# Seven-product x projections in the scan, with the sums of u kept on chip and gates and output halves staged in DRAM

## The chip, the cores and the metric

The kernel runs on one core of a Trainium2 chip. The metric is the device time of one execution in microseconds (us). Instructions of a core run on five engines with queues of their own: TensorE (PE, matmuls; PEld its weight loads), VectorE (DVE), ScalarE (ACT), GpSimd (POOL, here only an issuer of DMAs) and SyncE (SP, the issuer of the weight loads from DRAM).

## The reference

One layer of a hybrid decoder trunk over 512 tokens and 16 meta tokens (L = 528), width 1024, float32:

```python
u = rmsnorm(h, mix_norm_w[i])
proj = u @ w_in[i]              # 1024 x (1024 pool, 2048 z, 4096 xbc, 32 dt, 2048 gates)
gates = sigmoid(proj[..., OFF_GATE:] + b_gate[i])
y_pool = pool_mixer(u_pool, pool_w_group[i], pool_scale[i]) @ w_pool_up[i]
y_ssd = mamba2_branch(z, xbc, dt_raw, ...) @ w_ssd_out[i]    # 8 groups of 4 heads
h = h + (gate_pool * y_pool + gate_ssd * y_ssd) @ w_o[i]
v = rmsnorm(h, mlp_norm_w[i])
hid = relu(v @ w_ff1[i])
h = h + (hid * hid) @ w_ff2[i]
out = rmsnorm(h, final_norm_w)
```

In `mamba2_branch` each group has a B and a C tile of 128 columns, two x tiles of 128 and two z tiles. B, C and x go through a causal convolution of width 4 and a silu before the chunked scan.

## The kernel before

**Numbers as high and low parts.** Every float32 operand of a large matmul is split into a rounded part (ACT copy, `whi`) and the remainder (DVE subtraction, `wlo`). A product is three matmuls per 128-slice of the contraction: high by high, high by low, low by high.

**Stages.** (1) Squares, dt and the projections of group 0, with `first_raw` copies and the first four pool gates (`gate_pool(d, True)`); `norm_u` writes the normalised u as `uh` and `ul` (8 tiles each) and a copy to DRAM (`u_d`). (2) The scan: for each group g of 8, `ssd(g)` is interleaved by `weave` with the projections of group g+1 (`group_proj`), in group 4 also with the first half of the output product (`out_half`, contraction over ys 0 to 7), in group 7 with a further part (`out_part`). (3) The pool: two plain tiles, the last output slices (`psl`), then three pool pairs by seven products (`pool_pair`). (4) The merge of the branches and the output projection, (5) the MLP. In stages 4 and 5 products of 2 x 2 blocks are also formed by seven products in place of eight.

**Seven products.** Contraction and output columns are each cut in two, and so are the tokens. Seven products of sums of blocks, added up in the right order, replace eight block products. They need sums of the blocks of u (`sums_of_u`), and sums of the weight blocks. The latter are made by DMAs that accumulate in DRAM (`weight_sums`, on POOL's queue; a set of four sums is 8 DMAs, a set of two is 4), at the places given by `SETS_AT` (by group), `SETS_POOL` and a loop behind the merge. The sums of u are formed during groups 1, 2, 3 and 5 (`SUMS_AT`), written to DRAM (`t_d`) and loaded again ahead of the pool (`T`).

**Projections in the scan.** A plain tile (`proj`) multiplies 8 slices of a weight block with both halves of the tokens: 16 matmuls by `uh`, 16 by `ul`, 16 with `wlo`, each 264 columns wide (258 for C). The result lies in a PSUM tile of two banks (`psum2`, two such tiles) from which `conv` reads it. z and gate tiles are 512 columns wide.

**Order.** Each engine runs its instructions in one fixed order, which a list scheduler lays down when the kernel is built, by program order and its own times; `tc.issue_after(x)` keeps an instruction behind x. Weight blocks pass through three `raw`, four `whi` and four `wlo` buffers.

**Kept on chip.** Eight gate tiles `m1` (pool gates, 512 columns) and eight accumulators `acc` (the output product, 512 columns) lie in SBUF from the start of the scan or before. `out_half` copies into `acc` (ACT, line 636), `out_part` adds to it (DVE, line 665), `psl` adds the rest (line 898).

Of the kernel before, what the change touches and what calls it, by code (L numbers as in the profile page):

```python
# [47 lines left out]
SKIP = 8  # L48
TN = (L - SKIP) // 2

SUMS_AT = (1, 2, 3, 5)


SETS_AT = {0: 2, 1: 1, 3: 1, 5: 1, 6: 1}
# [9 lines left out]
def kernel(ctx: ExitStack, tc, xT, x, w, f1, f2, vec, fnw, out):  # L64
# [10 lines left out]
    nblk = [0]  # L75
# [66 lines left out]
    sel = const.tile([P, 2, P], F32, name="sel")  # L142
    dve.tensor_copy(sel[:, 0, :], ident[:, P - 1 : P].to_broadcast([P, P]))
    dve.tensor_copy(sel[:, 1, :], ident[:, NM - 1 : NM].to_broadcast([P, P]))
# [20 lines left out]

    gc_stack = ExitStack()
    gc = gc_stack.enter_context(tc.tile_pool(name="gc", bufs=2, side="left", reuse_waits="tile"))
    m1p = ctx.enter_context(tc.tile_pool(name="m1p", bufs=1, side="right", reuse_waits="tile"))
    m1 = [m1p.tile([P, SEQ], F32, tag=f"m1_{d}", name=f"m1_{d}") for d in range(NK)]
# [56 lines left out]
    wdt = pre.tile([P, NK, H], F32, name="wdt")  # L226
# [63 lines left out]
    dts_ = pre.tile([P, L], F32, name="dtp")  # L290
# [80 lines left out]
    def dt_out():  # L371

        pt = psum1("pt_dt")
# [17 lines left out]

    u_d = [dram.tile([P, 2 * TN], F32, name=f"u_d{k}") for k in range(NK)]

    def norm_u():
        for k in range(NK):
            dve.scalar_tensor_tensor(xt[k], xt[k], col(V_MIX, k), rsb, op0=ALU.mult, op1=ALU.mult)
            nc.gpsimd.dma_start(u_d[k], xt[k][:, SKIP:])
            act.copy(uh[k], xt[k])
            dve.tensor_tensor(ul[k], xt[k], uh[k].bitcast(F32), op=ALU.subtract)
# [19 lines left out]
    def first_raw(name, ps, skip):  # L419
        r = pre.tile([P, L - skip], F32, tag="raw0", name=f"raw0_{name}", bufs=4)  # L420
        act.copy(r, ps)
        dve.tensor_tensor(r, r, rsb[:, skip:], op=ALU.mult)
        return r

    def group_proj(g, cur, gate=None):
# [3 lines left out]
        for dst, t, skip in ((bt, 16 + g, 0), (ct, 24 + g, NM - 4), (xc[:, 0, :], 2 * g, 0),  # L429
                             (xc[:, 1, :], 2 * g + 1, 0)):  # L430
# [6 lines left out]
            yield  # L437
# [4 lines left out]
        for i in range(2):  # L442

            with tc.issue_after(done[0].ins) if g == 1 else nullcontext():
                wt = block()
            proj(narrow(ps[:, i * SEQ : (i + 1) * SEQ]), wt, X if first else U)
# [150 lines left out]

    def gate_pool(d, first=False):
        ps = psum2(f"pgp{d}")[:, :SEQ]
        proj(narrow(ps), block(), X if first else U)  # L600
        if first:
            dve.tensor_tensor(m1[d], ps, rsb[:, NM:], op=ALU.mult)
        act.activation(m1[d], m1[d] if first else ps, AF.Sigmoid, bias=col(V_BG, d))
# [17 lines left out]
    acc_stack = ExitStack()  # L621
    accp = acc_stack.enter_context(tc.tile_pool(name="accp", bufs=1, side="right", reuse_waits="tile"))
    acc = [accp.tile([P, SEQ], F32, tag=f"acc{d}", name=f"acc{d}") for d in range(NK)]
# [7 lines left out]
    def out_half():  # L631
        for dd in range(4):
            ps = psum2(f"pso{dd}")
            for i in range(2):
                ssd_out(2 * dd + i, ps[:, i * SEQ : (i + 1) * SEQ], range(8))
                act.copy(acc[2 * dd + i], ps[:, i * SEQ : (i + 1) * SEQ])
                yield

    def out_part():
# [24 lines left out]
        def add(ps, d):  # L664
            dve.tensor_tensor(acc[d], acc[d], ps, op=ALU.add)
# [14 lines left out]
        for d in range(2, NK):  # L680
# [8 lines left out]
    ts_stack = ExitStack()  # L689
    tsp = ts_stack.enter_context(tc.tile_pool(name="tsp", bufs=1, side="right", reuse_waits="tile"))  # L690
    t_d = {(n, p, k): dram.tile([P, 2 * TN], F32R, name=f"t_d{n}{p}{k}")
           for n in ("13", "42") for p in "hl" for k in range(4)}
    one, two = slice(0, TN), slice(TN, 2 * TN)

    B11, B12, B22, B21 = range(4)
    sets = [("f2", 0), ("f2", 1), ("f1", 0), ("f1", 1), ("f1", 2), ("f2", 2), ("f2", 3), ("f1", 3),
            ("f2", 4), ("f1", 4), ("f2", 5), ("f1", 5), ("f2", 6)]
    assert len(sets) == f1.shape[0] + f2.shape[0]  # L700
    SUMS = {"f1": ("t1", "s3", "t2", "t4"), "f2": ("t1", "s3")}
# [4 lines left out]
    def weight_sums():  # L706
        t = sets.pop(0)
        src = {"f1": f1, "f2": f2}[t[0]][t[1]]
# [22 lines left out]
    def sums_of_u(k, g):  # L731
        a, b = (tsp.tile([P, 2 * TN], F32, tag=t, name=f"{t}{k}") for t in ("ua", "ub"))

        with tc.issue_after(abc_load[g].ins):
            for t, kk in ((a, k), (b, k + 4)):
                sums_load[g] = nc.gpsimd.dma_start(t, u_d[kk])
        yield
        with tc.issue_after(masked[g].ins):
            dve.tensor_tensor(a[:, one], a[:, two], a[:, one], op=ALU.subtract)
            dve.tensor_tensor(a[:, two], b[:, two], a[:, two], op=ALU.subtract)  # L740
            dve.tensor_tensor(b[:, two], b[:, two], a[:, one], op=ALU.subtract)
            dve.tensor_tensor(b[:, one], b[:, one], b[:, two], op=ALU.subtract)
        yield
        for src, n in ((a, "13"), (b, "42")):
            hi, lo = (tsp.tile([P, 2 * TN], F32R, tag=f"t{p}", name=f"t{p}{n}{k}") for p in "hl")
            if n == "42":
                yield
            with tc.issue_after((y_first if n == "13" else squared)[g].ins):
                act.copy(hi, src)
            dve.tensor_tensor(lo, src, hi.bitcast(F32), op=ALU.subtract)  # L750
            nc.gpsimd.dma_start(t_d[n, "h", k], hi)
            nc.gpsimd.dma_start(t_d[n, "l", k], lo)
            yield

    for g in range(G):
# [4 lines left out]
        if g in SUMS_AT:  # L760
            fill.append(sums_of_u(SUMS_AT.index(g), g))
# [5 lines left out]
    ts_stack.close()  # L767


    gp_stack = ExitStack()  # L770
    gtp = gp_stack.enter_context(tc.tile_pool(name="gtp", bufs=2, side="left", reuse_waits="tile"))
    pool_stack = ExitStack()
    gp = pool_stack.enter_context(tc.tile_pool(name="gp", bufs=2, side="left", reuse_waits="tile"))
    tf = pool_stack.enter_context(tc.tile_pool(name="tf", bufs=1, side="left", reuse_waits="tile"))
# [34 lines left out]
    def pool_pair(p, behind=None):  # L809

        a1, a2 = raw_block(), raw_block()
        sm = tf.tile([P, 1024], F32, tag="sm", name=f"sm{p}")
# [3 lines left out]
        with tc.issue_after(behind[0].ins) if behind[0] is not None else nullcontext():  # L816
            dve.tensor_tensor(sm[:, h1], a2[:, h1], a2[:, h2], op=ALU.add)
        with tc.issue_after(behind[1].ins) if behind[1] is not None else nullcontext():
            dve.tensor_tensor(sm[:, h2], sm[:, h1], a1[:, h1], op=ALU.subtract)
        fs = split_form(sm, both, f"S{p}")  # L820
        dve.tensor_tensor(a1[:, h1], a1[:, h1], a2[:, h1], op=ALU.subtract)
        dve.tensor_tensor(a1[:, h2], a1[:, h2], sm[:, h2], op=ALU.subtract)
# [3 lines left out]
        x = psum2(f"pxx{p}")[:, :TN]  # L826
        y, z = (psum1(f"p{i}{p}")[:, :TN] for i in "yz")
        c1, c2 = slice(SKIP, SKIP + TN), slice(SKIP + TN, L)
        u1, u2 = (lambda k: (uh[k][:, c1], ul[k][:, c1])), (lambda k: (uh[k][:, c2], ul[k][:, c2]))
        form = lambda n, c: lambda k: (T[n, "h", k][:, c], T[n, "l", k][:, c])  # L830

        def product(*a):
            with tc.issue_after(last[p].ins) if p in last else nullcontext():
                multiply(*a)

        def multiply(ps, wf, c, f, start, stop, k0=0):
            for low in range(2):
                for k in range(4):
                    wt = wf[low][:, 512 * c + k * P : 512 * c + (k + 1) * P]
                    bh, bl = f(k0 + k)  # L840
                    last[p] = pe.matmul(ps, wt, bh, start=start and not low and k == 0,
                                        stop=stop and low == 1 and k == 3, skip_group_check=True)
                    if not low:
                        pe.matmul(ps, wt, bl, start=False, stop=False, skip_group_check=True)

        product(x, fa, 0, u1, True, False)
        act.copy(r1[:, c1], x)
        product(y, fa, 1, u1, True, True, 4)
        dve.tensor_tensor(r1[:, c1], r1[:, c1], y, op=ALU.add)
        product(x, fs, 1, form("42", two), False, False)  # L850
        act.copy(r1[:, c2], x)
        product(z, fs, 0, form("13", one), True, False)
        copied[p] = act.copy(r2[:, c2], z)
        product(x, fd, 0, form("13", two), False, False)
        dve.tensor_tensor(r2[:, c2], r2[:, c2], x, op=ALU.add)
        product(z, fd, 1, u2, False, True, 4)
        dve.tensor_tensor(r1[:, c2], r1[:, c2], z, op=ALU.add)
        first = averaged(2 * p, r1)
        product(x, fb, 1, form("42", one), False, True)
        act.copy(r2[:, c1], x)  # L860
        return [first, averaged(2 * p + 1, r2)]
# [55 lines left out]
    pool_stack.close()  # L917
    wo_stack = ExitStack()
# [735 lines left out]
```

## Time and profile before

| | |
|---|---|
| median of 3 runs | 1001.25 us (1000.6 to 1002.03) |
| profiled execution | 1001.49 us |
| its span, first to last instruction | 999.8 us |
| granted TensorE clock | 1.000 |
| PE busy | 991.7 us, 6095 matmuls |
| DVE, ACT, POOL busy | 790.8, 602.6, 88.3 us |
| scan, groups 0 to 7 | about 69 to 478 us |
| pool | about 478 to 558 us |

The profile is of one execution. Rows of instructions give a line of the kernel, the engine, the operation, the tile written and the tiles read, a count, the busy time and the mean duration; behind the bar stands the engine's idle time before them and what ended it. A line can be that of a helper. A matmul's own duration includes its way through the array; how fast matmuls follow one another is read from their starts, or from the chain, where each step counts only its part.

### The profile page before, as it was taken

The numbers are of one execution on the slowest core, as the hardware profiler recorded it, in microseconds if no ns is written. First come the engines' busy times: TensorE is split into PE (matmuls) and PEld (weight loads), VectorE is DVE, ScalarE is ACT, GpSimd is POOL, SyncE is SP. The second block draws the span as 40 slices with busy tenths as digits, with TensorE's granted clock in tenths as the row PEclk, the third lists the DMA queues.
The fourth block names the chain that finished last, engine by engine and source line by source line (L and its number), as shares of the span: only waits on it lengthen the run. The fifth ranks groups of instructions, "written<-read, shape, count | busy, mean of one in ns | idle before, by whom it ended". The sixth has DMA issues, their size and how long they took to land.

```text
span 999.8 us, 15519 instructions
## 1 busy us (share of the span) xinstructions
PE 991.7 (99%) x6095; PEld 879.2 (88%) x6095; DVE 790.8 (79%) x1141; ACT 602.6 (60%) x832; POOL 88.3 (9%) x148
## 2 busy tenths in 40 slices
PE   9999999999999999999999999999999999999997
PEld 7889999999889999988998888888889999999986
DVE  7988797979736687978789566976988888888885
ACT  8675958595827339483265433378666656656654
POOL 0022101111002011003210001121100000000000
PEclk9999999999999999999999999999999999999999
DMA  7378753677238635408988622879654455464432
GB/s 244 91 281 233 222 159 117 202 181 240 68 92 259 162 108 147 148 22 237 277 198 246 214 95 90 226 200 306 168 189 148 152 186 152 144 189 149 127 106 85
DMA packets 56203, 171.47 MB, mean 172 GB/s; under 512 B 6401, under 2 KB 7745, under 8 KB 55105
## 3 DMA queue, kind: packets, MB, share of 16 engines
q1 hardware_dynamic: 36576, 105.86, 32.4%
q0 software_dynamic: 18832, 63.71, 24.4%
q8 instruction: 48, 0.79, 0.3%
q10 hardware_dynamic: 720, 0.91, 0.3%
q14 instruction: 27, 0.21, 0.1%
HBM read 161.90 MB, written 48.40 MB: 210 GB/s over the span
## 4 chain that ended last, share of the span: by engine, by line
PE 96%; ACT 2%; DMA 0%; issue 0%; DVE 0%; SPq 0%; ACTq 0%
PE px L192 12%; PE px L1289 8%; PE alpha L1357 6%; PE px L194 6%; PE pz L192 5%; PE px L1292 4%; PE alpha L1360 3%; PE pgs L192 3%; PE pgp L192 3%; PE pz L194 3%; PE py L554 2%; PE po L548 2%; PE pf L128 1%; PE pf L127 1%; PE wo_alpha L1051 1%; PE pgp L194 1%
## 5 line engine op out<-in xcount | busy, mean ns | idle before, releaser
L93 ACT CAST whi<-raw 128x1024 fp32r<-128x1024 f32 (+2 forms) x98 | 98.5, 1015 | 105.3 <-PE px L194 31.8
L95 DVE TENSOR_TENSOR wlo<-raw,whi 128x1024 fp32r<-128x1024 f32 (+2 forms) x98 | 114.6, 1176 | 52.4 <-ACT whi L93 26.9
L192 PE MATMUL px<-uh,whi 128*128 128x264 f32 (+1 forms) x448 | 113.6, 291 | 0.0
L194 PE MATMUL px<-ul,whi 128*128 128x264 f32 (+1 forms) x448 | 110.7, 285 | 0.0
L192 PEld LDWEIGHTS px<-uh,whi 128*128 128x128 f32 x448 | 84.6, 189 | 1.8 <-issue 1.4
L194 PEld LDWEIGHTS px<-ul,whi 128*128 128x128 f32 x448 | 84.3, 188 | 0.4 <-issue 0.2
L1064 DVE TENSOR_TENSOR ht<-ht,alpha 128x1024 f32<-128x1024 f32 x35 | 42.7, 1219 | 29.1 <-PE alpha L1357 29.1
L987 ACT CAST shi<-rawf 128x1024 fp32r<-128x1024 f32 x42 | 44.2, 1053 | 28.6 <-PE alpha L1360 18.2
L192 PE MATMUL px<-uh,wlo 128*128 128x264 f32 (+1 forms) x448 | 58.5, 283 | 0.0
L192 PEld LDWEIGHTS px<-uh,wlo 128*128 128x128 f32 x448 | 55.9, 188 | 0.0
L1357 PE MATMUL alpha<-shi,hh 128*128 128x512 f32 x140 | 55.2, 394 | 0.0
L1360 PE MATMUL alpha<-shi,hl 128*128 128x512 f32 x140 | 54.7, 391 | 0.0
L988 DVE TENSOR_TENSOR slo<-rawf,shi 128x1024 fp32r<-128x1024 f32 x42 | 51.2, 1218 | 0.6 <-ACT shi L987 0.6
L1292 PE MATMUL px<-vsl,shi 128*128 128x256 f32 x192 | 47.4, 280 | 0.0
L1289 PE MATMUL px<-vsh,shi 128*128 128x256 f32 x192 | 47.4, 281 | 0.0
L194 PE MATMUL pz<-ul,whi 128*128 128x512 f32 x112 | 43.6, 389 | 0.0
L192 PE MATMUL pz<-uh,whi 128*128 128x512 f32 x112 | 43.6, 389 | 0.0
L575 DVE RECIPROCAL rs<-rs 128x128 f32<-128x128 f32 x32 | 27.2, 910 | 14.0 <-ACT rs L573 13.9
L1357 PE MATMUL alpha<-slo,hh 128*128 128x512 f32 x140 | 37.4, 389 | 0.0
L1289 PEld LDWEIGHTS px<-vsh,shi 128*128 128x128 f32 x192 | 36.2, 188 | 0.9
L1292 PEld LDWEIGHTS px<-vsl,shi 128*128 128x128 f32 x192 | 36.1, 188 | 0.9
L1292 PE MATMUL px<-vl,shi 128*128 128x256 f32 x144 | 36.1, 283 | 0.0
(558 smaller groups left out, 2856.8 us busy)
## 6 DMA issues: line engine op xcount, KB each, us to landing
raw<-in_w SPq DMA_DIRECT2D x104, 512.0 KB, 4.5
f_t<-in_f POOLq DMA_DIRECT2D x38, 512.0 KB, 6.6
f_s<-in_f POOLq DMA_DIRECT2D x26, 512.0 KB, 8.6
b<-in_f SPq DMA_DIRECT2D x21, 512.0 KB, 4.6
rawf<-in_f SPq DMA_DIRECT2D x36, 256.0 KB, 3.0
rawf<-f_t SPq DMA_DIRECT2D x36, 256.0 KB, 2.9
abc<-acs_d POOLq DMA_DIRECT2D x8, 1024.0 KB, 7.5
f_t<-f_t POOLq DMA_DIRECT2D x12, 512.0 KB, 4.4
```

Of the source, the lines that this page charges most:

```text
L93: act.copy(hi[:, c], raw[:, c])
L95: dve.tensor_tensor(lo[:, c], raw[:, c], hi[:, c].bitcast(F32), op=ALU.subtract)
L192: pe.matmul(o, wt, rhs[0][k][:, c], start=part == 0 and k == 0, stop=part == 1 and k == NK - 1)
L194: pe.matmul(o, wt, rhs[1][k][:, c], start=False, stop=False)
L575: dve.reciprocal(rs[:, ctok(c)], rs[:, ctok(c)])
L987: splits.append((act.copy(hi, src), dve.tensor_tensor(lo, src, hi.bitcast(F32), op=ALU.subtract)))
L988: dve.tensor_tensor(lo, src, hi.bitcast(F32), op=ALU.subtract)))
L1064: added[0] = dve.tensor_tensor(o, o, src, op=op)
L1289: pe.matmul(ps, m, f[k][0], start=start and not low and k == 0, stop=stop and low == 1 and k == 3, skip_group_check=True)
L1292: pe.matmul(ps, m, f[k][1], start=False, stop=False, skip_group_check=True)
L1357: pe.matmul(ps[t], hh[:, p, seg, st], m, start=bool(first and not low and p == 0), stop=bool(last and low and p == 1), skip_group_check=True)
L1360: pe.matmul(ps[t], hl[:, p, seg, st], m, start=False, stop=False, skip_group_check=True)
```

## The change

- The sums of u are formed during groups 0, 1 and 2 (two slices in group 2) in another arrangement of the seven products, with token halves of 264 in place of 260, and stay in SBUF (16 tiles `T`) up to the pool. The stores to and loads from `t_d` go.
- The two x tiles of groups 4 to 7 (projected during groups 3 to 6) are computed together by seven products (`pair`). Two PSUM banks take turns; ACT copies and DVE adds bring the products into two SBUF tiles (`ra`, `rb`), from which `conv` then reads both tiles. Two more weight sets (`fx`) of four sums each are formed, in groups 0 and 1; the other sets move back.
- Pool gates 0 to 6 and the output halves pass through a two-buffer staging tile (`gt`) to DRAM (`gate_d`, `acc_d`). The parts of group 7 are added by an accumulating DMA in place of the DVE add. After the scan `acc` and `m1` are loaded from DRAM.
- In group 0 the raw copies have three buffers for four, one shared with the dt product; the selection matrix is built later.

```diff
-SKIP = 8
-TN = (L - SKIP) // 2
-SUMS_AT = (1, 2, 3, 5)
-SETS_AT = {0: 2, 1: 1, 3: 1, 5: 1, 6: 1}
+SUMS_AT = {0: (0,), 1: (1,), 2: (2, 3)}
+X_PAIRS = (4, 5, 6, 7)
+BC_PAIRS = ()
+PAIRS = [(k, g) for g in range(G) for k in "bx" if g in (BC_PAIRS if k == "b" else X_PAIRS)]
+SETS_AT = {0: 1, 1: 1, 2: 1, 3: 1, 4: 1, 5: 1, 6: 1}
...
+    gtp = gp_stack.enter_context(tc.tile_pool(name="gtp", bufs=2, side="left", reuse_waits="tile"))
...
+    T = {(n, p, k): tf.tile([P, L], F32R, name=f"t{n}{p}{k}") for n in "01" for p in "hl" for k in range(4)}
...
-    m1 = [m1p.tile([P, SEQ], F32, tag=f"m1_{d}", name=f"m1_{d}") for d in range(NK)]
+    gate_d = [dram.tile([P, SEQ], F32, name=f"gate_d{d}") for d in range(NK)]
+    acc_d = [dram.tile([P, SEQ], F32, name=f"acc_d{d}") for d in range(NK)]
...
+    def factor_u(name):
+        if name in ("A11", "A12", "A22"):
+            o = 0 if name == "A11" else 4
+            c = HF[1] if name == "A22" else HF[0]
+            return [(uh[o + k][:, c], ul[o + k][:, c]) for k in range(4)]
+        n, c = {"S1": ("1", HF[1]), "S2": ("0", HF[0]), "S3": ("0", HF[1]), "S4": ("1", HF[0])}[name]
+        return [(T[n, "h", k][:, c], T[n, "l", k][:, c]) for k in range(4)]
+
+    MULTIPLY = (("b11", "A11", 0, True, False), ("b21", "A12", 1, True, True), ("t2", "S2", 0, False, False),
+                ("t1", "S1", 1, True, False), ("s3", "S3", 0, False, False), ("b22", "S4", 1, False, True),
+                ("t4", "A22", 0, False, True))
...
+    def pair(kind, g, r):
+        ps = psum2(f"pq{kind}{g}")
+        banks = (ps[:, :HALF], ps[:, 512 : 512 + HALF])
+        operands = pair_operands(PAIRS.index((kind, g)))
+        one, two = HF
+        for m, f, n, start, stop in MULTIPLY:
+            o = banks[n]
+            wt = next(operands)
+            f = factor_u(f)
+            for low in range(2):
+                for k in range(4):
+                    wk = wt[low][:, k * P : (k + 1) * P]
+                    pe.matmul(o, wk, f[k][0], start=start and not low and k == 0,
+                              stop=stop and low == 1 and k == 3, skip_group_check=True)
+                    if not low:
+                        pe.matmul(o, wk, f[k][1], start=False, stop=False, skip_group_check=True)
+            if m == "b11":
+                act.copy(r[0][:, one], o)
+            elif m == "b21":
+                dve.tensor_tensor(r[0][:, one], r[0][:, one], o, op=ALU.add)
+            elif m == "t2":
+                act.activation(r[1][:, one], o, AF.Copy, scale=-1.0)
+            elif m == "t1":
+                act.copy(r[1][:, two], o)
+                yield
+            elif m == "s3":
+                dve.tensor_tensor(r[1][:, two], r[1][:, two], o, op=ALU.subtract)
+            elif m == "b22":
+                dve.tensor_tensor(r[1][:, one], r[1][:, one], o, op=ALU.add)
+            else:
+                act.copy(r[0][:, two], o)
...
+    def staged(name):
+        return gtp.tile([P, SEQ], F32, tag="gt", name=name)
...
     def gate_pool(d, first=False):
...
-        act.activation(m1[d], m1[d] if first else ps, AF.Sigmoid, bias=col(V_BG, d))
+        act.activation(o, o if first else ps, AF.Sigmoid, bias=col(V_BG, d))
+        if d not in m1:
+            nc.gpsimd.dma_start(gate_d[d], o)
...
-                act.copy(acc[2 * dd + i], ps[:, i * SEQ : (i + 1) * SEQ])
+                o = staged(f"so{2 * dd + i}")
+                act.copy(o, ps[:, i * SEQ : (i + 1) * SEQ])
+                nc.gpsimd.dma_start(acc_d[2 * dd + i], o)
...
         def add(ps, d):
-            dve.tensor_tensor(acc[d], acc[d], ps, op=ALU.add)
+            o = staged(f"sp{d}")
+            act.copy(o, ps)
+            nc.gpsimd.dma_start(acc_d[d], o, accum_op=ALU.add)
...
+    sets = [("fx", n) for n in range(fx.shape[0])] + [
...
-            nc.gpsimd.dma_start(t_d[n, "h", k], hi)
-            nc.gpsimd.dma_start(t_d[n, "l", k], lo)
...
-        x = psum2(f"pxx{p}")[:, :TN]
-        y, z = (psum1(f"p{i}{p}")[:, :TN] for i in "yz")
+        c = psum2(f"pxx{p}")
+        c, z = c[:, :HALF], c[:, 512 : 512 + HALF]
+        y = psum1(f"py{p}")[:, :HALF]
...
-    T = {i: tf.tile([P, 2 * TN], F32R, name="t{}{}{}".format(*i)) for i in t_d}
-    for i, t in T.items():
-        t_load = nc.gpsimd.dma_start(t, t_d[i])
+    for d in range(NK):
+        t_load = nc.gpsimd.dma_start(acc[d], acc_d[d])
+    for d in range(NK - 1):
+        t_load = nc.gpsimd.dma_start(m1[d], gate_d[d])
```

More of the change, by code (lines that the diff above doesn't have):

```diff
@@ L836, in multiply @@
[L836 to L844, printed above, removed]
@@ L863, in pool_mix @@
+        product(z, fb, 1, "S4", False, True)
+        dve.tensor_tensor(r2[:, one], r2[:, one], z, op=ALU.add)
+        second = averaged(2 * p + 1, r2)
+        product(c, fd, 1, "A22", False, True)
+        act.copy(r1[:, two], c)
+        return [averaged(2 * p, r1), second]
     def pool_mix(gi, pooled, wgb):
```

246 lines of the change are left out of this document (159 added, 87 removed).

## The prediction

> **What bounds the kernel now.** I read the page first, then the list of waits of TensorE's weight loads, then the busy table cut at the turns of the eight scan groups, then the chain of waits and the timeline for the pace of one matmul.
>
> ```profile
> span 999.8 us, 15519 instructions
> PE 991.7 (99%) x6095; PEld 879.2 (88%) x6095; DVE 790.8 (79%) x1141; ACT 602.6 (60%) x832; POOL 88.3 (9%) x148
> PE   9999999999999999999999999999999999999997
> DVE  7988797979736687978789566976988888888885
> PE 96%; ACT 2%; DMA 0%; issue 0%; DVE 0%; SPq 0%; ACTq 0%
> ```
>
> TensorE is busy in every slice and is 96% of the chain that ended last. A busy TensorE need not be one at full pace, so the second view asks what its weight loads ever waited for:
>
> ```profile
> PEld pso L127 <- ACT acc L636: 0.6, 2, 0.4
> ...
> PEld pxx L841 <- DVE pu L855: 0.2, 1, 0.2
> ```
>
> The columns are the total, the number of times and the longest. Behind the start-up no single wait is longer than 0.4 us. So there is nothing to win by removing a wait: the time can only fall if matmuls fall, and any new wait of TensorE is added in full. The profiled execution took 1001.49 us, 1.69 more than its span; the median of the three timed runs is 1001.25, 0.24 below it. I work out a difference and put it on the median. About 0.2% (2 us) is what a measurement of this kernel can tell from no change.
>
> **The matmuls that go and the ones that widen.**
>
> ```profile
> 231.09 1.93 PE px L192 x16
> ...
> 504.86 0.29 PE L841 MATMUL pxx<-uh,whiA 128*128 128x260 f32 x1
> ...
> 514.89 0.28 PE L841 MATMUL pxx<-uh,whiA 128*128 128x260 f32 x1
> ```
>
> The first row is of the chain: 16 matmuls of 264 columns in 1.93 us, 120.6 ns apiece. A plain x tile is 8 slices of the contraction, two column halves and three matmuls each (high by high, high by low, low by high): 48, so 96 for a pair. Seven products of 4 slices and three matmuls are 84. Twelve go in each of four pairs: 48 x 120.6 ns = **5.79 us** taken away, all on the path, and 6095 matmuls become 6047.
> The Trainium skill ("TensorE: Matmul & The Clock Gate", Back-to-back issue gap) gives N/2.4 + 2.5 ns for a warm matmul; by that 264 columns would take 112.5 ns, an estimate, and the term would be 5.4 us. The row is slower than the page and decides.
>
> In the pool the seven products exist already and only widen from 260 to 264 columns. The timeline's two rows are the starts of two pool pairs: 84 matmuls in 10.03 us, 119.4 ns. Three pairs are 252 matmuls. At 120.6 against 119.4 ns that is 0.3 us; by columns alone (4/264 of 120.6 ns each) 0.46. I take **+0.3**.
>
> **What the pair costs the other engines.**
>
> ```profile
> L93 ACT CAST whi<-raw 128x1024 fp32r<-128x1024 f32 x92 | 95.9, 1051 | 105.3 <-PE px L194 31.8 <-DMA raw<-in_w 18.3 <-PE pso L128 17.7
> L95 DVE TENSOR_TENSOR wlo<-raw,whi 128x1024 fp32r<-128x1024 f32 x92 | 111.8, 1219 | 52.4 <-ACT whi L93 26.9 <-PE px L192 7.6 <-PE pz L192 6.2
> L855 DVE TENSOR_TENSOR pu<-pu,pxx 128x260 f32<-128x260 f32 x3 | 1.2, 417 | 0.0
> L851 ACT COPY pu<-pxx 128x260 f32<-128x260 f32 x3 | 1.1, 372 | 2.5 <-PE pxx L841 2.5
> 232.24 0.42 DVE L739 TENSOR_TENSOR ua<-ua 128x260 f32<-128x260 f32 x1
> 240.04 0.62 ACT L749 CAST th<-ua 128x520 fp32r<-128x520 f32 x1
> 240.69 0.70 DVE L750 TENSOR_TENSOR tl<-ua,th 128x520 fp32r<-128x520 f32 x1 [0.68 <-ACT th L749]
> ```
>
> Seven half blocks of weights are split in place of two whole ones: 1.5 more splits, 1.58 us of ACT and 1.83 of DVE. Four copies (ACT, 0.372) and three adds (DVE, 0.417) take the products out of PSUM: 1.49 and 1.25 us. A pair thus adds **3.1 us to each engine**. One slice of the sums of u is four DVE operations and two forms, 4 x 0.42 + 2 x 0.70 = 3.1 us of DVE and 1.2 of ACT. These move from groups 1, 2, 3, 5 to 0, 1, 2, 2. So on DVE the turns of groups 3 and 5 come out even, and turns 0, 2 and 6 gain about 3.1 us:
>
> ```profile
> 68.84:111.80 42.96, 42.96 (x321) 40.20 (x320) 32.16 (x53) 29.49 (x38) 9.39 (x14) 1.00 0.94 275
> ...
> 160.30:209.04 48.74, 48.74 (x347) 44.85 (x347) 39.72 (x65) 35.39 (x46) 7.25 (x13) 1.00 0.56 168
> 209.04:257.62 48.58, 48.58 (x345) 44.71 (x344) 40.02 (x64) 35.99 (x47) 5.45 (x9) 1.00 0.65 180
> ...
> 388.00:431.70 43.70, 43.70 (x321) 40.44 (x320) 35.61 (x55) 30.52 (x39) 0.57 (x1) 1.00 0.31 96
> 431.70:477.80 46.10, 46.10 (x255) 38.60 (x254) 40.83 (x56) 24.25 (x32) 9.58 (x18) 1.00 0.55 164
> ```
>
> The columns are the turn's length, then busy PE, weight loads, DVE, ACT and POOL. The tightest is the turn of group 6: DVE 35.6 + 3.1 = 38.7 us in 43.7 - 1.46 = 42.2. It fits, at 92%. As totals the engines hide the work; the cost, if any, comes from its place.
>
> **The hand-over inside a pair.** In the scan pair two PSUM banks take turns, and a product that accumulates onto a bank may start only when the copy or add of the last result in it is done. In between runs one product, 12 x 120.6 ns = 1.45 us. There are five such hand-overs in a pair, 20 in all: three of a pair's on ACT, two on DVE. The trace of before has this very situation in its three pool pairs, four hand-overs each, on a DVE as full as the scan's:
>
> ```profile
> 228.00:240.00 12.00, 12.00 (x108) 11.71 (x107) 11.71 (x20) 3.95 (x5) 1.18 (x2) 1.00 0.86 246
> ...
> 398.00:406.00 8.00, 8.00 (x71) 7.55 (x70) 8.00 (x12) 6.23 (x8) 0.00 (x0) 1.00 0.00 0
> ...
> 520.00:540.00 20.00, 20.00 (x135) 18.34 (x134) 19.47 (x29) 10.65 (x17) 3.51 (x5) 1.00 0.84 204
> ```
>
> Twelve hand-overs at a DVE 97% busy cost 0.2 us together (the L855 wait above). At that rate 20 cost 0.3. At the other end each finds one low-half split in front: 1.219 + 0.417 - 1.45 = 0.19 us, 3.7 in all. DVE is 98 to 100% busy in the scan's windows, so I take neither end but near the pool's row, **+1.0 us**.
> The convolution of both x tiles now follows the whole pair, under the two z blocks:
>
> ```profile
> 421.00:432.00 11.00, 11.00 (x51) 9.07 (x50) 5.25 (x13) 10.11 (x12) 0.00 (x0) 1.00 0.30 107
> ```
>
> DVE has 5.7 us free there for the three steps that come later. ACT, busy 10.1 of 11, has not much for the first tile's two activations; the next transposes need them only behind the z blocks, so I take 0 and return to it below.
>
> **DMA and queues.** POOL's queue loses 32 stores and loads of the sums and gains 16 for the two new weight sets, 7 gate stores, 8 stores and 8 accumulates of the output halves and 15 loads: 22 more, on a queue 9% busy. What can hurt is order, since a POOL issue that waits holds those behind it.
>
> ```profile
> t_d13h<-th POOLq DMA_DIRECT2D x4, 260.0 KB, 2.5
> t13l<-t_d13l POOLq DMA_DIRECT2D x4, 260.0 KB, 5.0
> ...
> 103.35 0.83 POOL L713 DMA_DIRECT2D f_t<-in_f  x1 [5.67 <-DMA f_t<-in_f]
> 109.84 0.54 POOL L716 DMA_DIRECT2D f_t<-f_t  x1 [4.35 <-DMA f_t<-in_f]
> ...
> 466.44 0.63 DVE L665 TENSOR_TENSOR acc<-acc,psp 128x512 f32<-128x512 f32 x1
> ...
> 474.35 0.69 DVE L665 TENSOR_TENSOR acc<-acc,psp 128x512 f32<-128x512 f32 x1 [1.72 <-PE psp L130]
> ...
> 496.29 1.30 DVE L898 TENSOR_TENSOR acc<-acc,psl 128x512 f32<-128x512 f32 x2
> ```
>
> An accumulating DMA of 512 KB was waited for up to 6.5 us (103.35 to 109.84); the new ones carry 256 KB. The staging tile has two buffers, and ACT needs one back after two products of group 7, 7.9 us (466.44 to 474.35), so the accumulate is hidden. The last one can end by 474.35 + 0.6 + 6.5 = 481.5 and its load 5.0 later, at 486.5; the last add that needs it runs at 496.29. Some 10 us of cover; without it the delay is paid by TensorE, whose products have four banks. The gates are not needed until the merge. In group 4 an output half's store (2.5 us) may sit behind an accumulate chain of the weight sets, also about 6.5 us:
>
> ```profile
> 380.44 2.04 PE pz L192 x9
> ```
>
> That is 9.0 us in a ring that allows two half products, and one is 24 matmuls of 512 columns at 227 ns (2.04 us over 9), 5.4 us. So 0 is taken, with a few us as the other end. Copies in place of DVE's adds in group 7 ease DVE, whose time no TensorE wait shows, so that earns nothing. The weight sets move back by one in the sequence, the raw copies of group 0 get three buffers for four, and the selection matrix is built later: each waits on things done well before TensorE asks; 0.
>
> **Sum:** -5.79 + 0.3 + 1.0 = -4.5 us: the profiled execution would take 997.0 and the median **996.8 us**.
>
> **The rivals.**
> *Hand-overs queue on DVE (slower).* Two splits in front of an add in a pair make it 2 x 1.219 + 0.417 - 1.45 = 1.4 us late; in all eight DVE hand-overs that is 11.3 us, net +5.8: 1007. It outweighs the gain once the 20 hand-overs lose 0.27 us each on average (5.49/20). For it: DVE without a gap at 398 to 406, and banks that alternate more tightly than the pool's, whose second result has a bank of its own. Against it: the 0.2 us of the pool pairs, and z blocks and scan products that can be ordered between. The Trainium skill ("PSUM — Partial Sum Buffer", PSUM bank collisions raise a hardware error) says that no engine may read a bank while TensorE writes it, in whatever columns; so such a wait cannot be overlapped within a bank. The trace agrees as far as its L855 wait goes.
> *ACT is full at the turns, above all into group 4 (gain partly lost).*
>
> ```profile
> 250.00:258.00 8.00, 8.00 (x39) 6.63 (x38) 3.93 (x6) 7.88 (x13) 0.00 (x0) 1.00 0.08 33
> 257.00:268.00 11.00, 10.95 (x60) 9.08 (x59) 8.98 (x16) 10.94 (x19) 0.00 (x0) 1.00 0.16 46
> ```
>
> ACT (fifth figure) has no slack there and TensorE waited 0.6 us for L636. If ACT holds that turn, the first pair's 1.45 us is lost: -3.0, 998.2; each further turn that it holds takes as much. Against: two forms (1.2 us) leave that turn, and TensorE waited for nothing of ACT's at the others.
> *The staging is late (slower).* If POOL's order puts accumulates or loads 18 us later than above, TensorE pays the 8 us beyond the cover: +3.5, 1004.8. Against: nothing else fills POOL's queue in group 7.
> *It evens out:* hand-overs at the 0.27 us of the break-even, 1001.
>
> **How the numbers follow.** Forecast 0.54, ACT at the turns 0.16, even 0.07, DVE hand-overs 0.17, staging 0.06. Faster is the first two, 0.70; same 0.07; slower 0.23. The range runs from no hand-over loss (-5.79 + 0.3, less 0.7 for the runs' own spread) at 995.0 up to 1003.5, which takes in the lighter third of the slower cases and leaves out some 0.17 above and 0.03 below. The likeliest case's own range is 995.0 to 998.5.
>
> **What would show it.** 6047 matmuls; px groups with 48 fewer; products of a pair 1.45 us apart in the timeline of groups 3 to 6, with no idle time of the weight loads put down to the pair's copies and adds; each of those turns 1.45 us shorter. Idle time ahead of the second, third or fourth product, released by DVE, is the first rival; idle in the first products of the output half, released by ACT, the second; idle ahead of the psl products, released by a DMA through DVE, the third. The forecast is wrong if the weight loads' waits in the scan add up to over 3 us.

## The result, and the profile after

The changed kernel takes 1048.54 us (median of 4 runs, 1048.28 to 1049.20) against 1001.41 for the kernel before: a ratio of 1.0471, 95% interval 1.0454 to 1.0488. It is **slower by 47 us**, where 4.5 us less were forecast. Of the profile of the changed kernel, the span, the busy times, TensorE's row of slices and the chain that ended last:

```profile
span 1047.5 us, 15589 instructions
PE 1002.9 (96%) x6047; PEld 880.4 (84%) x6047; DVE 800.2 (76%) x1153; ACT 616.6 (59%) x863; POOL 105.3 (10%) x170
PE   9999699999899998899998999999999999999997
PE 72%; ACT 9%; DVE 7%; DMA 6%; issue 4%; POOL 1%; SPq 0%; POOLq 0%; ACTq 0%; DVEq 0%
```

The 48 matmuls did go (6047), yet TensorE was busy 11 us longer, and idle 45 us in place of 8. Its row of slices shows where: one slice of 6 at 105 to 131 us, and a string of 8s. What the weight loads waited for (total, times, longest), rows left out that are small:

```profile
PEld ptm L578 <- ACT xc L416: 8.6, 2, 6.6
PEld po L646 <- DVE st L635: 5.9, 5, 1.4
PEld pst L625 <- ACT btok L575: 5.8, 2, 4.2
PEld pxx L958 <- DVE pu L974: 4.5, 2, 3.4
PEld ptx L586 <- DVE xddm L579: 4.2, 3, 3.4
PEld pso L128 <- ACT whi L94: 3.8, 1, 3.8
PEld pxx L958 <- ACT pu L968: 2.1, 3, 0.7
...
PEld pqx L475 <- DVE rbx L491: 1.4, 3, 0.9
```

The waits named after a pair's own copies and adds (pqx) are small. The large ones belong to the scan's next step: ACT or DVE is late with something that stands further back in its queue. The stages are cut at the first transposition of each group's B (ptb) in the timeline: the turn of a group runs from its own to the next group's, turn 7 up to the first plain product of the pool (pp), and the start ends at group 0's. The pool is counted from the first psl to the first pup product:

| us | start | turn 0 | 1 | 2 | 3 | 4 + 5 | 6 | 7 | pool |
|---|---|---|---|---|---|---|---|---|---|
| before | 68.8 | 43.0 | 48.7 | 48.5 | 48.6 | 130.4 | 43.7 | 42.5 | 68.5 |
| changed | 70.7 | 43.3 | 60.7 | 48.6 | 51.7 | 137.6 | 53.9 | 44.0 | 81.0 |

The loss is in turns 1, 3, 4 + 5 and 6 and in the pool, with 1.5 to 2 us each at the start and in turn 7. The stretch from the first pp to the first psl product (11.66 us) and the merge (76.16, from the first pup product) are as before, and what follows the merge is 1.1 us shorter. Turn 1 has no pair in it at all.

**Turn 1** is read from GpSimd's queue, here of the changed kernel:

```profile
72.65 0.54 POOL L709 DMA_DIRECT2D gate_d<-gp  x1 [4.49 <-ACT gp L707]
...
74.27 0.54 POOL L812 DMA_DIRECT2D fx_t<-in_fx  x1
...
104.27 0.81 POOL L820 DMA_DIRECT2D fx_t<-in_fx  x1 [4.26 <-DVE sqg L664]
104.80 0.85 POOL L566 DMA_DIRECT2D abc<-acs_d  x1
```

and of the kernel before:

```profile
62.81 0.54 POOL L711 DMA_DIRECT2D f_t<-in_f  x1
...
94.94 0.59 POOL L468 DMA_DIRECT2D abc<-acs_d  x1 [7.30 <-PE py L554]
```

Before, two short weight sets began at 62.81, and the load of group 1's decay sums (abc) waited only for its buffer. After, one long set, eight DMAs of which most wait for an earlier one, begins behind a gate's store and two loads of u at 74.27 and issues its last at 104.27: abc goes out 9.9 us later. Then ACT, in order, holds everything behind its first reader:

```profile
116.76 1.28 ACT L597 ACT_TABLE_LOAD   x1 [11.91 <-DMA abc<-acs_d]
118.05 1.06 ACT L597 ACTIVATE eb<-abc 64x1024 f32<-64x1024 f32 x1
119.13 1.28 ACT L416 ACT_TABLE_LOAD   x1
120.42 0.64 ACT L416 ACTIVATE xc<-xc 128x528 f32<-128x528 f32 x1
```

The silu of the x tile (xc), whose last input DVE had finished at 107.3 us, stands behind that exponential, and TensorE's next transposition needs it. TensorE's timeline and its busy times in the two stretches behind the stall (length, PE, PEld, DVE, ACT, POOL, then the granted clock):

```profile
121.12 0.48 PE L578 MATMUL ptm<-ident,xc 128*128 128x128 f32 x1 [6.41 <-ACT xc L416]
...
127.13 0.42 PE L197 MATMUL px<-ul,whi 128*128 128x264 f32 x1
127.35 0.42 PE L195 MATMUL px<-uh,whi 128*128 128x264 f32 x1
121.00:128.00 7.00, 3.77 (x16) 3.48 (x17) 4.17 (x10) 6.92 (x8) 2.18 (x4) 0.50 0.53 172
128.00:135.00 7.00, 7.00 (x53) 6.95 (x53) 5.83 (x8) 6.96 (x16) 1.97 (x3) 0.92 0.79 158
```

After 6.4 us of idling the granted clock (the share of its full speed that TensorE is given) is 0.50, and matmuls of 264 columns start 0.22 us apart, where the prediction's row had 0.12. A stall is thus paid a second time, though at a lower price: the clock was 0.50 from 118.9 to 129.1 us, TensorE was busy for 4.9 us of these, and half of that, 2.5 of the 12.0 us of turn 1, is the most that the clock can have cost, by my estimate. In the whole run the half clock held for 20.5 us, 14.5 of them busy: at most 7.2 of the 47 us.

### The profile page after: what moved, and what is told of

Read it like the earlier page. It is cut to its first block, busy times and chain, and to the rows that moved or that the text cites. A ratio compares the mean times of both kernels' runs of the same rounds, so it can differ in the third digit from the quotient of the medians.

```text
span 1047.5 us, 15589 instructions
## 1 busy us (share of the span) xinstructions
PE 1002.9 (96%) x6047; PEld 880.4 (84%) x6047; DVE 800.2 (76%) x1153; ACT 616.6 (59%) x863; POOL 105.3 (10%) x170
## 4 chain that ended last, share of the span: by engine, by line
PE 72%; ACT 9%; DVE 7%; DMA 6%; issue 4%; POOL 1%; SPq 0%; POOLq 0%; ACTq 0%; DVEq 0%
PE px L1408 8%; PE alpha L1476 6%; PE px L195 5%; PE px L1411 4%; PE alpha L1479 3%; PE px L197 3%; PE pgs L195 3%; DMA abc<-acs_d 3%; DMA raw<-in_w 2%; PE pso L128 2%; PE wo_alpha L1170 1%; PE pso L129 1%; PE pf L129 1%; PE pf L128 1%; PE pqx L475 1%
## 5 line engine op out<-in xcount | busy, mean ns | idle before, releaser
L94 ACT CAST whi<-raw 128x1024 fp32r<-128x1024 f32 (+2 forms) x90 | 90.1, 1011 | 79.1 <-PE pso L129 15.7
L96 DVE TENSOR_TENSOR wlo<-raw,whi 128x1024 fp32r<-128x1024 f32 (+2 forms) x90 | 104.9, 1172 | 39.0 <-ACT whi L94 27.6
L195 PE MATMUL px<-uh,whi 128*128 128x264 f32 (+1 forms) x320 | 82.0, 294 | 0.0
L197 PE MATMUL px<-ul,whi 128*128 128x264 f32 (+1 forms) x320 | 79.9, 287 | 0.0
L195 PEld LDWEIGHTS px<-uh,whi 128*128 128x128 f32 x320 | 61.4, 192 | 1.4 <-issue 0.9
L197 PEld LDWEIGHTS px<-ul,whi 128*128 128x128 f32 x320 | 61.1, 191 | 0.2
L1107 DVE TENSOR_TENSOR slo<-rawf,shi 128x1024 fp32r<-128x1024 f32 x42 | 51.1, 1218 | 0.6 <-ACT shi L1106 0.6
L197 PE MATMUL pz<-ul,whi 128*128 128x512 f32 x112 | 43.7, 390 | 0.0
L195 PE MATMUL px<-uh,wlo 128*128 128x264 f32 (+1 forms) x320 | 41.8, 283 | 0.0
L195 PEld LDWEIGHTS px<-uh,wlo 128*128 128x128 f32 x320 | 39.9, 188 | 0.0
L1411 PEld LDWEIGHTS px<-vsl,shi 128*128 128x128 f32 x192 | 36.1, 188 | 0.9
L1411 PE MATMUL px<-vl,shi 128*128 128x256 f32 x144 | 36.1, 283 | 0.0
L1408 PE MATMUL px<-vh,shi 128*128 128x256 f32 x144 | 36.0, 282 | 0.0
```

What stands on the lines that cost most here:

```text
L94: act.copy(hi[:, c], raw[:, c])
L96: dve.tensor_tensor(lo[:, c], raw[:, c], hi[:, c].bitcast(F32), op=ALU.subtract)
L195: pe.matmul(o, wt, rhs[0][k][:, c], start=part == 0 and k == 0, stop=part == 1 and k == NK - 1)
L197: pe.matmul(o, wt, rhs[1][k][:, c], start=False, stop=False)
L1408: pe.matmul(ps, m, f[k][0], start=start and not low and k == 0, stop=stop and low == 1 and k == 3, skip_group_check=True)
L1411: pe.matmul(ps, m, f[k][1], start=False, stop=False, skip_group_check=True)
```

## The experiments

The first theory was the queue: GpSimd's DMAs are late and hold ACT. Its rival was the pairs themselves.

**The decay load on another queue.** `abc_load[g] = nc.sync.dma_start(...)` in place of `nc.gpsimd`.

> The changed kernel, with the load of the decay sums (abc, 1 MB per group) issued from SyncE's queue in place of GpSimd's. Queue theory: in the turn of group 1 the load of group 1 stood behind the stores and the eight chained weight-sum DMAs on GpSimd's queue, ACT waited 11.9 us for it and TensorE behind ACT; so the turn of group 1 falls from 60.7 us to 49 to 52, the turn of group 6 by 2 to 5, and the time to 1030 to 1038. Rival, the pairs' own load on ACT and DVE: both turns keep their length within 3 us, time 1045 to 1049.

1059.35 us, ratio 1.0575 (1.0544 to 1.0606). A miss: start 91.1 and turn 0 56.4 us, though turns 1, 3, 6 and 7 were 50.1, 48.0, 44.8 and 42.5. With the load of group 0 back on GpSimd's queue (`nc.sync if g else nc.gpsimd`):

> The changed kernel with the load of the decay sums on SyncE's queue from group 1 on; that of group 0, which there stood behind 45 us of weight loads in the first trial, stays on GpSimd's. Queue theory: the start and the turn of group 0 as in the changed kernel (70.7 and 43.3 us), the turns of groups 1, 3, 6 and 7 as in the first trial (50, 48, 45 and 42.5), so 25 us off: 1021 to 1026. Rival, the shorter turns of the first trial were only work done early during its long start: the turn of group 1 is again over 55 us and the time over 1035.

1067.15 us (1.0654; 1.0614 to 1.0695): start 89.5, turn 0 69.1, turn 1 50.0. Turn 1 is as the theory said and the time is not. GpSimd's queue shows why:

```profile
1.34 0.67 POOL L812 DMA_DIRECT2D f_t<-in_f  x1 [0.33 <-issue]
...
73.28 2.02 POOL L373 DMA_DIRECT2D acs_d<-dacs  x4
...
109.36 0.87 POOL L566 DMA_DIRECT2D abc<-acs_d  x1
```

The sets of turns 3 to 6 had been held in place by the decay loads ahead of them in the same queue. Without these, they ran from the start, ahead of the store of the decay sums (46.89 us in the changed kernel, here 73.28) and the load of group 0 (67.61 in the changed kernel, here 109.36). So most of the loss was moved rather than removed. Why turn 6 is short here (45.5) is not shown: it is not only that no set is left for it, for a run below without sets in turns 5 and 6 has 51.1. A second run of that kernel:

> A second run of the kernel with the load on SyncE's queue from group 1 on, for the spread of its stages: turns within 1 us of the first run's.

1067.62 us; turns within 0.6 us of the first run's except 4 (1.5), the start 2.3 apart.

**The sums and the pairs, one at a time.** Without the x sets: `src = fx[s, quadrant]` for every product, so the sums of the weights are left out, and with them the sets of the first two turns. Without pairs: `X_PAIRS = ()`, the set lists kept; then both dropped.

> The changed kernel with its pairs, but the two weight sets of the x pairs are not made: each product reads a single quadrant in place of a sum, so the 16 sum DMAs of the turns of groups 0 and 1 are gone and nothing else (the result is left wrong in groups 4 to 7). Queue theory: turn of group 1 at 49 to 52 us in place of 60.7, the turns of groups 4 to 7 as in the changed kernel within 3 us together, time 1033 to 1038. Rival, the pairs themselves: time 1045 to 1049.

> The changed kernel with x tiles of groups 4 to 7 as plain projections, as in the kernel before; the sums of u (needed in the pool) and the weight sets (now unused) are still made and all staging stays. 48 matmuls return, +5.8 us. Queue theory: turn of group 1 stays at 60 us and the pool part 12 us longer than before; the late half-block weight loads of groups 5 and 6 are gone; time 1036 to 1044. Rival, the pairs' load on ACT and DVE and their hand-overs cause most of it: time 1008 to 1025.

> As the run without pairs, and the two weight sets of the x pairs are not made either. Queue theory: turn of group 1 falls to 49 to 52 us; time 1024 to 1033, what is left being the pool part (12 us), the turn of group 6 and the start. Rival, pairs alone: the same time as the run without pairs within 3 us.

1038.12 (1.0363; 1.0333 to 1.0393), 1027.86 (1.0260; 1.0231 to 1.0290) and 1021.20 us (1.0194; 1.0112 to 1.0277). The first time is at the edge of what the queue theory said; the other two are below it, so the theory gave the pairs too small a share. Without sets turn 1 is 48.7 us, the time of the kernel before: the queue theory holds for turn 1 and for nothing else. Without pairs (48 matmuls more!) turns 4 + 5 and 6 return to 130.5 and 43.3, while turn 3 stays at 53.1 and 54.4. The pool stayed at 78.7 to 81.9 us in all three. With the sets but without pairs turn 1 is 55.0, not 60.7, and this too is the load: it landed 2.7 us behind the start of turn 1 in the changed kernel and 4.3 us ahead of it here, and in every run in which it landed 9 us or more ahead, turn 1 takes 48.7 to 50.5.

**The pool.** `c, z = psum2 halves` back to `c = psum2(...)[:, :HALF]` and `z = psum1(...)`; and `SETS_POOL = 0`.

> The changed kernel with the second result of the pool's pairs in a PSUM tile of its own, as in the kernel before, in place of the second half of the first one's tile. If the shared tile holds TensorE up in the pool (it waited 4.5 us for DVE's last add there): the part from the psl products to the first pup product falls from 81.0 us to 70 to 75, time 1037 to 1042. If the pool waits for late weight loads: 79 to 81 us there, time 1046 to 1049.

> The changed kernel with the three weight sets of the pool part made later, behind the loads of x at the end of the merge: 24 DMAs less beside the pool's weight loads. If late weight loads hold the pool up: that part falls from 81.0 us to 69 to 74, and the rest stays or grows by a few us for sets that come late, time 1036 to 1045. If it is the shared PSUM tile: 80 to 82 us there and the time 1046 to 1052.

1035.48 us (1.0338; 1.0223 to 1.0453), the pool at **69.2**; and 1042.45 us (1.0408; 1.0283 to 1.0533), the pool at 75.8. The tile alone restores the pool to 0.7 us of before, with the sets where they were; moving the sets takes off 5.1 us, between the two answers, and leaves the rest. Of the pool's waits in the list above, 0.6 us is left with an own tile.

The timeline shows what differs. The product t1 is the first of its pair to write its bank. With the shared tile, then with its own:

```profile
545.78 0.39 ACT L968 ACTIVATE pu<-pxx 128x264 f32<-128x264 f32 x1 [1.28 <-PE pxx L958]
546.23 0.39 PE L958 MATMUL pxx<-t1h,whiS 128*128 128x264 f32 x1 [0.48 <-ACT pu L968]
```

```profile
548.12 0.29 PE L957 MATMUL pz<-t1h,whiS 128*128 128x264 f32 x1
548.32 0.39 ACT L967 ACTIVATE pu<-pxx 128x264 f32<-128x264 f32 x1 [1.28 <-PE pxx L957]
```

The ACT rows copy the result of the product before t1 out of the *other* bank. With one tile for both banks t1 waits until that copy is done; with its own it starts before the copy does. The scan's pairs have the form of the shared tile: six such waits in a pair, each for the reader of the product just ended.

**The order mended.** Own tile in the pool; `SETS_AT = {0: 1, 1: 1, 4: 1}` with a short set first and the long x sets in turns 1 and 4; all four pairs, none, or those of 5 and 6.

> The changed kernel, all four pairs, with three repairs: the pool pair's second result in a tile of its own; one short weight set (four DMAs, f2) in the turn of group 0, the two long x sets in the turns of groups 1 and 4 and none in 2, 3, 5 and 6; the rest made at the end of the merge. Queue theory: turn of group 1 at 48.7 to 50 us (60.7 in the changed kernel), of group 3 at 48 to 50 (51.7), of group 6 at 44 to 47 (53.9), the pool at 68.5 to 70 (81.0); left over are the turn into group 4, where ACT is full (turns 4 and 5 together 134 to 138 against 130.4 before): 1008 to 1015. Rival, the pairs' own work on ACT and DVE makes the turns long wherever the sets stand: turn of group 6 over 50, time over 1020.

> As the run with all repairs, but no pairs and no x sets: short weight sets in the turns of groups 0 and 4 alone. What is left of the change is the sums of u kept on chip and the gates and output halves waiting in DRAM. Queue theory: every turn within 0.5 us of the kernel before except the start (+1.5 to 2.5) and the turn of group 0 (+0 to 1.7); 1001 to 1006. Rival, the two u loads with one buffer in the turn of group 2 hold up turn 3 whatever the sets do: that turn at 52 us or more, time over 1006.

> As the run with all repairs, with pairs in groups 5 and 6 alone, which are built in the two long turns of groups 4 and 5; one x set in the turn of group 1. If only the place of the pairs (the turn into group 4) and the order of the DMAs cost, these two pairs earn their 2.9 us: 2 to 3 us below the run with repairs and no pairs. If each pair costs more on the weight loads and on ACT than it saves wherever it stands: the same time or up to 8 us above.

1020.79 (1.0180; 1.0159 to 1.0201), 1004.20 (1.0022; 1.0013 to 1.0032) and 1011.88 us (1.0097; 1.0082 to 1.0112). With all pairs turn 1 is 50.5, turn 3 48.0, the pool 68.8, but 4 + 5 stay at 137.9 and 6 at 51.1: here the rival was right. Without pairs every turn and the pool are within 0.7 us of before. Two pairs in the middle of long turns do not earn 2.9 us but lose 7.7, and 6.3 of it in turn 6 behind them (49.6 against 43.3). So something in the pair itself costs, and two runs were made to tell the shared tile from ACT's work, and one for a single pair:

`banks = (psum2(...)[:, :HALF], psum1(...)[:, :HALF])`; `conv(..., silu=False)` for paired tiles; `X_PAIRS = (5,)`.

> The run with all repairs and all four pairs (1020.8 us), with the two results of a scan pair in two PSUM tiles in place of the two halves of one; as the program has it, a product then waits for the last reader of its own result and not for that of the product directly before it. Theory, ACT's queue at the turns: the 4 us of TensorE's waits for the pairs' copies and adds go, turns 4 and 5 together stay at 136 to 138 and the turn of group 6 at 49 to 51; 1015 to 1020. Rival, the hand-overs inside the pair make everything behind them late: turns 4 and 5 below 133, turn 6 below 46, time 1003 to 1011.

> The run with all repairs and all four pairs, with the last step of the convolution (silu) left out for the eight x tiles of the pairs: two activations of 0.64 us and one or two table loads of 1.28 us less on ACT at each of four turns, nothing else. Theory, ACT's queue at the turns: TensorE's waits for btok and for the first half's split fall by 2.5 to 4 us at the turns into groups 4 and 6, and the slow stretches behind them with them: 1006 to 1014. Rival, late weight loads or hand-overs on DVE: under 3 us less, 1017 to 1021.

> The run with all repairs, with the pair of group 5 alone (one x set, in the turn of group 1). This pair stands in the middle of a long turn. If a pair there earns its 12 products of 120.6 ns: 1.0 to 1.8 us below the run without pairs (1004.2), 1002.4 to 1003.2. If each pair costs more than that wherever it stands: 1004.2 to 1007.

**1005.57** us (1.0035; 1.0020 to 1.0051), 1007.23 (1.0055; 1.0035 to 1.0075) and 1007.14 (1.0054; 1.0038 to 1.0071). Two tiles take off 15.2 us, leaving turns 4 + 5 at 132.6 and 6 at 42.3: the hand-overs. The single pair in a shared tile costs, with its weight set, 2.9 us even in the middle of a long turn, 2.0 of it in turns 4 + 5. Leaving out the silu takes off nearly as much, 13.6, with turns 4 + 5 at 131.6 and 6 at 45.3. The two results fit together in ACT's timeline ahead of group 4, with one shared tile:

```profile
249.51 0.35 ACT L493 COPY rax<-pqx 128x264 f32<-128x264 f32 x1
249.76 0.83 ACT L411 ACTIVATE xc<-rbx,vs 128x528 f32<-128x528 f32 x1
...
269.73 1.98 ACT L94 CAST whi<-raw 128x1024 fp32r<-128x1024 f32 x2
```

and with two:

```profile
242.78 0.82 ACT L411 ACTIVATE xc<-rbx,vs 128x528 f32<-128x528 f32 x1
243.94 0.38 ACT L492 COPY rax<-pqx 128x264 f32<-128x264 f32 x1 [0.34 <-PE pqx L474]
...
265.61 1.04 ACT L94 CAST whi<-raw 128x1024 fp32r<-128x1024 f32 x1
```

The pair's last result leaves PSUM 5.6 us later, the first convolution begins 7.0 later, and ACT, full at that turn, reaches the split of the first output half's weights 4.1 later. TensorE idles and then runs slowly. One tile, then two, the same stretches (the seventh figure is the granted clock, 0.72 in the second row):

```profile
264.00:270.00 6.00, 1.99 (x8) 1.44 (x8) 1.64 (x3) 5.97 (x10) 0.86 (x1) 1.00 0.45 98
270.00:276.00 6.00, 5.19 (x16) 4.14 (x17) 6.00 (x6) 2.92 (x4) 0.00 (x0) 0.72 0.65 160
```

```profile
264.00:270.00 6.00, 6.00 (x31) 4.91 (x30) 4.12 (x8) 5.97 (x10) 1.17 (x2) 1.00 0.73 119
270.00:276.00 6.00, 5.94 (x27) 4.61 (x26) 5.90 (x7) 3.66 (x5) 1.06 (x2) 1.00 0.61 184
```

The tile makes the pair late, and ACT's full queue carries the delay to TensorE; slackening either one takes most of it away.

**Do the two causes add up, and what is left?** The changed kernel with the tiles alone; then order and tiles with the stores of gates and output halves, or of the halves alone, on ACT's queue (`nc.scalar.dma_start`).

> The changed kernel with its own places of the weight sets, and only the PSUM tiles mended: two tiles for the results of a scan pair and a tile of its own for the second result of a pool pair. If the shared tile and the order of the DMAs add up: pool 69 us, turns 4 and 5 together 131 to 134, turn 1 still 60 us, 1020 to 1025. If the order of the DMAs only hurts because the pairs have no slack: turns 1, 3 and 6 within 1 us of the kernel before, 1004 to 1010.

> The run with all repairs and the pairs' two tiles (1005.6 us), with the stores of the gates and output halves issued from ACT's queue, behind the activation that makes each, in place of GpSimd's. If the store that stood behind a chain of accumulating DMAs (9.3 us to land, TensorE 3 us idle in the first output halves) is what is left in turn 4: turns 4 and 5 together at 129 to 130.5, 1001.5 to 1003.5. If ACT pays for the issues at its full turns: 1005 or more.

> As the run before, but only the stores of the output halves are issued from ACT's queue, those of the gates from GpSimd's. If the gates' stores cost nothing on either queue: within 0.7 us of the run before.

**1013.28** (1.0121; 1.0099 to 1.0143), 1001.97 (1.0005; 0.9996 to 1.0014) and **1000.67** us (0.9998; 0.9987 to 1.0010). The first lies between its two answers and the second fits; the last was to be within 0.7 us of the second and is 1.3 below it, with overlapping intervals, so what the gates' stores cost on either queue is not settled. The tiles alone take off 35 us:

| us | start | turn 0 | 1 | 2 | 3 | 4 + 5 | 6 | 7 | pool | span |
|---|---|---|---|---|---|---|---|---|---|---|
| changed | 70.7 | 43.3 | 60.7 | 48.6 | 51.7 | 137.6 | 53.9 | 44.0 | 81.0 | 1047.5 |
| order and pool tile | 70.7 | 43.3 | 50.5 | 48.6 | 48.0 | 137.9 | 51.1 | 44.0 | 68.8 | 1019.3 |
| tiles alone | 70.5 | 43.3 | 60.8 | 48.5 | 49.2 | 128.3 | 42.4 | 43.5 | 69.1 | 1011.4 |
| order and tiles | 70.7 | 43.3 | 50.1 | 48.5 | 47.8 | 132.6 | 42.3 | 43.5 | 69.1 | 1003.8 |
| and halves by ACT | 70.5 | 44.9 | 50.5 | 48.5 | 47.8 | 127.9 | 42.3 | 43.5 | 68.8 | 1000.5 |

Turn 1 needs the order, the rest the tiles; turns 3 and 6 are shortened by either, turn 6 mostly by the tiles. The 4.3 us that the mended order gave back in turns 4 + 5 is one store, behind the second x set that was moved there:

```profile
274.94 0.55 POOL fx_t L819
275.48 9.32 DMA acc_d<-so
...
285.54 0.71 PE pso L128
```

The rows are of the chain with order and tiles mended. ACT waits for the staging buffer that this store still reads, and TensorE for ACT. On ACT's queue the store does not stand there, and turns 4 + 5 fall by 4.6 us.

**The first set ahead of the scan**, at 25 us, held back by two small stores.

> The run with all repairs, the pairs' two tiles and the output halves' stores on ACT's queue (1000.7 us), with the first long weight set made at 25 to 55 us, where the DMA engines were 0 to 0.3 busy, in place of the turn of group 1; two stores of 2 KB hold it back until then. If what is left in the turn of group 1 (50.5 us, 48.7 before) is that set: that turn at 48.7 to 49.2, start and turn of group 0 as in that run (70.5 and 44.9) or 1 us longer, 998 to 1000. If the set delays the stores that the first decay load reads: the start or turn 0 is 2 us or more longer and the time 1001 to 1005.

1007.02 us (1.0048; 1.0034 to 1.0062): the second answer, 2 us beyond its range. Turn 1 came to 49.2, but turn 0 to 50.1: the chain took until 60 us, and the store of the decay sums stood behind it:

```profile
59.67 0.82 POOL L732 DMA_DIRECT2D fx_t<-in_fx  x1 [4.66 <-DMA fx_t<-fx_t]
60.21 2.31 POOL L373 DMA_DIRECT2D acs_d<-dacs  x4
```

The best version is level with the kernel before; none is shown to beat it.

## Why the prediction was wrong

**Only matmuls can win, new waits count in full:** right, and not strong enough. A long wait also slows the clock behind it, here by at most 7.2 us in all (estimated above).

**The 48 products (-5.79), the wider pool (+0.3):** both fit. The 48 matmuls went. With everything mended, turns 3 to 7 take 261.5 us against 265.9 without pairs: -4.3, where -5.79 + 1.0 was forecast; no run measures the two terms apart, and against the kernel before (265.1) it is -3.6. The mended pool is 68.75 to 69.2 us against 68.49, +0.3 to +0.7.

**The hand-over (+1.0, ends 0.3 and 3.7): the step that failed most.** It said that a product may start when the last result *in its bank* is out, with one product of 1.45 us in between, and took the pool pairs of the kernel before as proof. Those had three tiles. The change puts two banks into one tile, in the scan and in the pool, and the program then orders products and readers by the tile: no product lies between. In the changed kernel, with its order left as it is, the price was 36.1 us of span (1047.5 to 1011.4): 11.9 in the pool, 2.5 in turn 3, 9.3 in 4 + 5, 11.5 in 6. That the pool's second result moves into the first one's tile stood in the diff, and the first rival even names the bank of its own that it had before, but the pool was costed by its columns alone.

**The convolution behind both tiles (0):** ACT "has not much" there, and the second rival priced a late turn at 1.45 us. The place was right and so was the sign: TensorE idle in the first output half, released by ACT, 3.8 us. The price was wrong: by the run without pairs, turns 4 + 5 lost 7.4 us with the order mended. The delay was the shared tile's, ACT's full queue passed most of it on (4.1 us of 5.6), and the clock added to it.

**DMA and queues (0, "a few us as the other end"): the second failure.** "What can hurt is order" was the right sentence with no number behind it. The sequence of the sets was not walked through: the first set became a long one, eleven microseconds later, ahead of a load that ACT needs. That is 12.0 us in turn 1, of which the new order took back 10.6. The store behind an accumulating chain was foreseen, at 9.0 us to land in a ring that allows 5.4, and put at 0. It landed after 9.32 us, and it hurt where the mended order put a set: TensorE was idle for 3.0 us, and with the stores on ACT's queue turns 4 + 5 are 4.6 us shorter.

**The rivals:** the first went the right way by another mechanism; its sign, waits on DVE inside the pairs, stayed small (1.4 us for L491, the largest). The third did not happen: pp to psl is 11.66 us in both kernels, so the cover of 10 us held. **The bound of 3 us** on the scan's waits, beyond which the forecast would be wrong, was passed at once: the five scan rows shown with more than 3 us each add up to 28.3.

**Left open:** the start is 1.4 to 2.5 us longer than before in every version whose sets stay in their places, with or without pairs, and turn 0 went to 44.9 in the best one. No run separates the three raw copies from the later selection matrix or the u stores. This is why the best version is only level: up to the end of turn 2 it is 5.2 us behind the kernel before (214.3 against 209.0), and the pool costs it 0.3 more, while turns 3 to 7 earn 3.6 and the shorter end 1.2.

## What to carry to other kernels

Before counting a hand-over as hidden, look which *tile* the two results lie in: in this program banks that share a tile alternate without overlap, and the waits then appear somewhere else, in the next stage of an engine with a full in-order queue. Where a queue of DMAs is refilled, write the new sequence down with its times, above all each chain whose DMAs wait for each other, and look for the first thing behind it that another engine needs. An unanswered "order can hurt" is a cost without a number, not a zero.

## What the runs showed of the hardware

A TensorE stall is followed by a stretch at half pace: TensorE was without work from 114.7 to 121.1 us, the granted clock was 0.50 from 118.9 to 129.1, and matmuls of 264 columns then came 0.22 us apart, against 0.12 at a clock of 1.00. The Trainium skill ("TensorE: Matmul & The Clock Gate", Part 1, The HAM clock gate) says that an idle window of about 3.4 us halves the clock and a busy one of that length restores it. The trace agrees with the halving and, roughly, with the length: the clock fell 4.2 us after the last matmul and came back 3.3 us after steady work had set in at 125.8.

A small DMA right behind a large accumulating one on the same queue was late rather than slow: the store of 256 KB, with a median of 3.8 us from issue to landing, was issued at 275.48 us, 0.54 behind an accumulating DMA of 512 KB. That one landed at 283.60 and the store at 284.80, after 9.32 us.

```profile
acc_d<-so POOLq DMA_DIRECT2D x8, 256.0 KB, 3.8
```

The row is of the run with order and tiles mended. The Trainium skill ("DMA: Bandwidth & Descriptors", Anatomy of one DMA, SWDGE path) fits 2.0 us plus the bytes at 436 GB/s, 2.6 us for 256 KB by my estimate; the trace is above that even at the median.
